# Three heads' gated outputs transposed by 32x32 blocks and a trip through memory, and the first transposes of the probabilities issued before the next scores

## The chip, the cores and the metric

The kernel is one program on one core of a Trainium2 chip. The core has five engines that each run their own list of instructions in order and wait for one another through semaphores: PE (TensorE, matrix products and transposes by a product with the identity, results to PSUM), DVE (VectorE), ACT (ScalarE), POOL (GpSimd) and SP (SyncE, which here only issues DMAs). PEld is the row of the profile that shows the loading of PE's stationary operand; it runs beside PE.

The metric is the device time of one execution in microseconds (us). The kernel before was timed three times: 1155.04, 1155.28 and 1155.72 us, median 1155.28. Its profiled execution took 1155.31 us, of which 1153.3 us lie between the first and the last instruction that the profile shows (the span). All times of rows below are in us from the start of that span, unless marked ns.

## The reference, cut to what matters

Two layers over 512 tokens of width 1024. Layer 1 is retention with four heads, chunked, here computed for all 512 tokens at once; layer 2 is attention with four groups of four heads, each head over all earlier tokens of two branches (selected blocks, which at this length are all of them, and a window of 512), plus a compressed branch.

```python
def retention_layer(h, g_norm, w_in, gn_gain, w_out):
    proj = rmsnorm(h, g_norm) @ w_in
    q, k, v, gate = jnp.split(proj, [...], axis=-1)
    ...
    o = retention_chunkwise(q, k, heads(v, RET_V_DIM))
    o = (o - mu) * lax.rsqrt(var + EPS) * gn_gain
    y = (jax.nn.silu(gate) * o).astype(h.dtype) @ w_out
    return h + y

def nsa_query_block(q, gates, blk, k_cmp, v_cmp, k_sel, v_sel, k_win, v_win):
    ...
    p_s = softmax(where(valid_s, q @ ks * scale, NEG)); o_s = p_s @ vs
    ...
    p_w = softmax(where(valid_w, q @ kw * scale, NEG)); o_w = p_w @ vw
    return gates[..., 0:1] * o_c + gates[..., 1:2] * o_s + gates[..., 2:3] * o_w
```

## The kernel before, in words

**Products.** Every operand of a product is held as a high and a low part in a four-byte format; `mm3` (L349) issues three products per pair (high-high, high-low, low-high). Weights come through one stream of 512 KB pieces: `Stream.load` issues the DMA on SP into one of four raw buffers, POOL multiplies a gain in where the piece needs one (L176, two halves), ACT writes the high part (L190, or L194 by slices with the gain) and DVE the low part (L205, or L209). `W.tick()` does one such step ahead of need; `W.tick(2)` does two.

**Order.** Nothing is scheduled by a tool: the order in which the code is written is the order on each engine. PSUM has eight banks under four tags: "d" two banks, "s" three, "pt" two, "o" one. A bank under a tag is taken in turn, and the product that writes it again waits until DVE or ACT has read what was there.

**Layer 1.** For head h the code computes q and k (`proj_rot`, four calls of 24 products of 128x512, the results read from "d" by `rot_mul` on DVE), then adds the output projection of head h-1 (`out_proj`), then v, the scores, the gate and the output of head h (`retention_out`, whose last instruction, L514 on POOL, leaves y = gate times the normalized output in `gate[:, t]`, 128 tokens by 512). The output projection needs y with its features on the partitions. `retention_yT(t)` does this: four PE transposes of 128x128 into a "pt" bank (L519), then `split_psum` (ACT copies the high part, DVE subtracts the low part) into `yH` and `yL`. For heads 1 to 3 these four calls (for the head before) stand between the calls of `proj_rot`; for the last head they stand after the loop.

**Layer 2.** The loop at L1034 runs over four groups and eight steps u in each; u = 2h + b is head h and branch b. One step holds: `scores(next)` for the following step (products into three "s" banks; DVE adds the mask, L942 and L945, and takes the row maximum, L947; ACT takes the exponential into `P`, L954); up to three fillers from a list (`fill(0)`, `fill(1)`, `fill(2)`: pieces of projections of 12 products each, which go to "d" banks); `scale_probs(next)` (DVE reciprocal, L963, then POOL scales the four parts of `P`, L967); `probs_T(u, 0)` and `probs_T(u, 1)`, the PE transposes of the scaled probabilities of this step (L976: eight into both "pt" banks, then two into one) with their splits (ACT L364, DVE L365) into `tH`, `tL`; `W.tick(2)`; in even steps `cmp_T(h)`, four more transposes into "pt" (L906), read by ACT (L909) and DVE (L910); then `values(u)`, the products of probabilities and values into "o" (L355, in odd steps first one of L984), read in odd steps by DVE and ACT (L993 to L995).

**Fillers.** What the three fillers are depends on the step. A gate or query projection is two fillers that fill one "d" bank, read by ACT and DVE (L752 and L753, L739 and L740) after the second. A piece of the output projection of the group before (`pair_tiles`) is two fillers that each fill two "d" banks, read by DVE (L1015). Seven steps have pieces of an output projection as both of the first two fillers: step 5 of group 0, steps 1 and 5 of groups 1 to 3. Steps with only two fillers have none between `cmp_T` and `values`: steps 0 to 3 and 7 of group 0, step 7 of groups 1 and 2, and steps 2, 4, 6 and 7 of group 3; step 3 of group 3 has one.

Of the kernel before, what the change touches and what calls it, by code (L numbers as in the profile page):

```python
# [11 lines left out]
F32 = mybir.dt.float32  # L12
F32R = mybir.dt.float32r
BF = mybir.dt.bfloat16
AF = mybir.ActivationFunctionType
# [221 lines left out]
def decoder(ctx: ExitStack, tc: tile.TileContext, x, xT, stream, cst, msk, gains, fnorm, out):  # L237
    nc = tc.nc
    pe, act, dve, pool = nc.tensor, nc.scalar, nc.vector, nc.gpsimd
    ctx.enter_context(tc.manual_schedule())  # L240
    sb = ctx.enter_context(tc.tile_pool(name="sb", bufs=1))
    ps = ctx.enter_context(tc.tile_pool(name="ps", bufs=1, space=bass.MemoryType.PSUM))
    nF = 4096 + 1024 * RAWS + 700 + 8192
    nR = 8192 + 2048 * SLOTS + 15104
# [4 lines left out]
    def V(o, n):  # L249
        assert o + n <= nF, (o, n)  # L250
        return arenaF[:, o:o + n]
# [12 lines left out]
    fb = 4096 + 1024 * RAWS  # L264
# [44 lines left out]
    yH = R(rb + 10752, 2048).rearrange("p (c n) -> p c n", c=4)  # L309
    yL = R(rb + 12800, 2048).rearrange("p (c n) -> p c n", c=4)  # L310
# [3 lines left out]
    cs = V(fb + 4096, 1024).rearrange("p (a n) -> p a n", a=2)  # L314
    dec = V(fb + 5120, 1024).rearrange("p (h n) -> p h n", h=2)
    yb = [V(fb + 6144 + 512 * i, 512) for i in range(2)]
    rx = V(fb, 4096).rearrange("p (k t n) -> p k t n", k=NK, t=NT)


# [5 lines left out]
    o = psum("o")  # L325
# [83 lines left out]
    def proj_rot(h, b, c):  # L409
        p = W.get("rin", 0, 1024, b + 256 * h + 128 * c, 128)  # L410
        o = psum("s" if h == 0 and b else "d")
        wst(p, o, 0, 4)
        if h or c == 0:
            W.tick()
        wst(p, o, 4, 8)
        p.done()
        if h == 0:
            return o
        rot_mul(o, c)
# [6 lines left out]
    def rot_split(H, L):  # L426
        pool.tensor_sub(rot[:, 0], rot[:, 0], rot[:, 3])
        pool.tensor_add(rot[:, 1], rot[:, 1], rot[:, 2])
        for i in range(2):
            c = slice(512 * i, 512 * i + 512)  # L430
            act.activation(H[:, c], rot[:, i], AF.Copy)
            dve.tensor_sub(L[:, c], rot[:, i], H[:, c].bitcast(F32))
# [83 lines left out]
    def retention_yT(t, bank="pt"):  # L516
        p = psum(bank)
        for c in range(4):
            pe.transpose(p[:, 128 * c:128 * c + 128], gate[:, t, 128 * c:128 * c + 128], ident)  # L519
        p3 = p.rearrange("p (c n) -> p c n", c=4)  # L520
        c = slice(128 * t, 128 * t + 128)
        split_psum(yH[:, :, c], yL[:, :, c], p3)

    def out_tile(t, c, p, YH, YL):
        o = psum("s" if t % 2 else "d")
        for a in range(2):
            mm3(o, [(YH[:, 2 * a + k, 128 * t:128 * t + 128], YL[:, 2 * a + k, 128 * t:128 * t + 128],
                     p[a].h[:, k], p[a].l[:, k]) for k in range(2)], a == 0, a == 1)
        d = hacc[:, t, 512 * c:512 * c + 512]
        dve.tensor_add(d, d, o)  # L530
# [15 lines left out]
    for h in range(HEADS):  # L546
        if h == 0:
            p = [W.get("rin", 0, 1024, 128 * c, 128) for c in (0, 1)]
            o = [psum("d") for c in (0, 1)]
            for k in range(NK):  # L550
                for c in (0, 1):
                    wst(p[c], o[c], k, k + 1)
                if k % 4 == 3:
                    W.tick()
            for c in (0, 1):
                p[c].done()
            dve.tensor_copy(masks, yb[0][:, :M_END])
            o += [proj_rot(h, 1024, c) for c in (0, 1)]
            rotary_scale()
            for b in range(2):  # L560
                for c in range(2):
                    rot_mul(o[2 * b + c], c)
                rot_split(*((kH, kL) if b else (qH, qL)))
        else:
            proj_rot(h, 0, 0)
            retention_yT(0)
            retention_yT(1)
            proj_rot(h, 0, 1)
            rot_split(qH, qL)
            retention_yT(2)  # L570
            retention_yT(3)
            proj_rot(h, 1024, 0)
            proj_rot(h, 1024, 1)
            rot_split(kH, kL)
            run(out_proj("rout", h - 1, yH, yL))
        tokens("rin", h, 2048, v_evac, ("o", "s", "pt", "pt") if h == 0 else ("d", "d", "s", "s"))
        retention_scores(h)
        if h < 3:
            load_decay(h + 1)
        tokens("rin", h, 4096, g_evac, ("d", "d", "pt", "pt"))  # L580
        for t in range(NT):
            retention_out(t)
# [258 lines left out]
    p = v_pieces(0)  # L841
# [127 lines left out]
    def probs_T(u, part, tag="pt"):  # L969
        Pu = P[u % 2]  # L970
        for j0, bank in (((0, (0,)), (1, (1, 3))), ((2, (2,)),))[part]:
            p = psum(tag)
            f = 0
            for j in bank:
                for i in range(j, NT):
                    pe.transpose(p[:, f:f + 128], Pu[:, PO[i] + 128 * j:PO[i] + 128 * j + 128], ident)  # L976
                    f += 128
            c = slice(TO[j0], TO[j0] + f)
            split_psum(tH[:, c], tL[:, c], p[:, :f])
# [54 lines left out]
    for g in range(GROUPS):  # L1034
        f = fillers(g)
        for u in range(8):
            h = u // 2
            last = (g, u) == (3, 7)
            W.auto = False
            left = 2 * len(between(g, h))  # L1040
            first = 4 if h == 3 else left // 2
            n = PLAN[u] if g == 3 else left - first if u % 2 else first
            steps = [1, 1, 0] if last else PARTS[n]

            def fill(i):
                for _ in range(steps[i]):
                    next(f)

            sums = None
            if u < 7:  # L1050
                nxt = g, u + 1
            elif g < 3:
                k_proj(g + 1, 0)
                k_proj(g + 1, 1)
                nxt = g + 1, 0
            else:
                nxt = None
            if g == u == 0:
                fill(0)
            if nxt:  # L1060
                sums, chain = scores(*nxt)
            if g or u:
                fill(0)
            if sums is not None:
                scale_probs(*nxt, sums)
            probs_T(u, 0)
            next(chain, 0)
            fill(1)
            probs_T(u, 1, "pt" if steps[1] else "d")
            W.tick(0 if last else 2)  # L1070
            next(chain, 0)
            if u % 2 == 0:
                cmp_T(h)
            fill(2)
            if u % 2 == 0:
                o_head = psum("o")
            values(g, u, o_head)
            W.auto = True
        run(f)
        if g < 3:  # L1080
            p = v_pieces(g + 1)
            for t in range(NT):
                v_proj(g + 1, t, p, ("d", "pt")[t % 2], t % 2)
# [101 lines left out]
```

## Time and profile before

| | |
|---|---|
| Median of three runs | 1155.28 us |
| Profiled execution, device time | 1155.31 us |
| Its span | 1153.3 us |
| PE busy | 1132.1 us (98%), 5812 products and transposes |
| DVE busy | 710.4 us (62%) |
| ACT busy | 486.7 us (42%) |
| POOL busy | 317.4 us (28%) |
| Memory traffic | 101.90 MB, mean 88 GB/s |
| PE transposes of L519 (y) | 64, of which 48 before the last head's |
| PE transposes of L976 (probabilities) | 320, in 32 steps |

A matrix product's row starts when it starts and ends when its last result is out, so rows that follow each other overlap; how long PE takes for a piece of work is read here from the start of its row to the start of the next row of PE. In brackets at the end of a row stands how long the engine had been idle before it, and who ended that.

### The profile page before, as it was taken

Reading aid. Unit: us, or ns where it says so; the run is one execution under the profiler, and the core shown is the slowest. Engines: PE = TensorE matmul, PEld = TensorE weight load, DVE = VectorE, ACT = ScalarE, POOL = GpSimd, SP = SyncE. Lnnn points to the kernel's source line nnn. Section 1 sums busy time; section 2 is a strip of 40 time slices with the busy share of each in tenths; the row PEclk is TensorE's granted clock in tenths of the full one; section 3 lists DMA queues with packets and bytes.
Section 4 is the critical chain, followed back from the end, with each engine's and each line's share of the span. In section 5 each row is a group of like instructions: output and inputs, shape, how many; then the busy total and the mean of one; then the engine's idle time right before and its main releaser. Section 6 shows DMA issues by size and latency. Waiting matters only on the chain. (4 is left out here: it accounts for less than half of the span.)

```text
span 1153.3 us, 15259 instructions
## 1 busy us (share of the span) xinstructions
PE 1132.1 (98%) x5812; PEld 964.3 (84%) x5812; DVE 710.4 (62%) x1226; ACT 486.7 (42%) x916; POOL 317.4 (28%) x357
## 2 busy tenths in 40 slices
PE   9999999999999999999899999999999999999997
PEld 7888888888888888988777889888898888988886
DVE  4746435544634665656577865778468774788555
ACT  6433223223323454545455433444345443444653
POOL 0212003002200212346645332354153431421012
PEclk9999999999999999999999999999999999999999
DMA  8422331222232123244531211222031211221211
GB/s 329 149 97 73 110 101 55 92 101 74 86 116 73 55 78 106 73 152 160 163 110 56 74 37 39 78 85 66 27 93 55 74 56 44 85 85 44 74 37 73
DMA packets 29593, 101.90 MB, mean 88 GB/s; under 512 B 3536, under 2 KB 3792, under 8 KB 29520
## 3 DMA queue, kind: packets, MB, share of 16 engines
q1 hardware_dynamic: 29088, 100.15, 26.8%
q8 instruction: 45, 0.74, 0.3%
q10 hardware_dynamic: 432, 0.79, 0.2%
q14 instruction: 28, 0.23, 0.1%
HBM read 98.83 MB, written 2.10 MB: 88 GB/s over the span
## 5 line engine op out<-in xcount | busy, mean ns | idle before, releaser
L355 PE MATMUL d<-arenaR 128*128 128x512 f32 (+2 forms) x2904 | 676.5, 386 | 2.4 <-ACT arenaR L136 1.0
L355 PEld LDWEIGHTS d<-arenaR 128*128 128x128 f32 x2904 | 524.5, 188 | 103.2 <-DVE arenaF L753 1.4
L355 PE MATMUL s<-arenaR 128*128 128x512 f32 (+8 forms) x1182 | 239.8, 354 | 0.7 <-ACT arenaR L364 0.5
L205 DVE TENSOR_TENSOR arenaR<-arenaF,arenaR 128x1024 fp32r<-128x1024 f32 (+1 forms) x142 | 191.7, 1369 | 70.5 <-ACT arenaR L190 70.3
L355 PEld LDWEIGHTS s<-arenaR 128*128 128x128 f32 x1182 | 200.3, 188 | 30.6 <-ACT arenaR L364 0.7
L190 ACT ACTIVATE arenaR<-arenaF 128x1024 fp32r<-128x1024 f32 (+1 forms) x142 | 145.8, 1048 | 105.6 <-PE s L355 68.4
L176 POOL TENSOR_TENSOR arenaF<-arenaF 128x512 f32<-128x512 f32 x108 | 135.3, 1276 | 99.2 <-DMA arenaF<-stream_dram 94.7
L355 PE MATMUL o<-arenaR 128*128 128x512 f32 (+3 forms) x744 | 128.8, 322 | 6.3 <-DVE arenaR L792 4.1
L967 POOL TENSOR_SCALAR arenaF<-arenaF 128x512 f32<-128x512 f32 (+3 forms) x128 | 67.2, 545 | 232.3 <-ACT arenaR L364 118.8
L355 PEld LDWEIGHTS o<-arenaR 128*128 128x128 f32 x744 | 114.3, 189 | 19.6 <-DVE arenaR L792 5.1
L954 ACT ACTIVATE arenaF<-s,arenaF 128x512 f32<-128x512 f32 (+3 forms) x128 | 67.1, 526 | 101.4 <-DVE arenaF L947 90.6
L365 DVE TENSOR_TENSOR arenaR<-pt,arenaR 128x512 fp32r<-128x512 f32 (+1 forms) x141 | 82.9, 618 | 36.9 <-ACT arenaR L364 34.3
L364 ACT ACTIVATE arenaR<-pt 128x512 fp32r<-128x512 f32 (+1 forms) x141 | 70.8, 541 | 73.3 <-PE pt L976 35.2
L371 POOL TENSOR_TENSOR arenaF<-arenaF 128x1 f32<-128x1 f32 (+1 forms) x25 | 14.2, 570 | 295.3 <-DVE arenaF L370 295.3
L355 PE MATMUL pt<-arenaR 128*128 128x512 f32 (+1 forms) x384 | 75.9, 349 | 0.0
L355 PEld LDWEIGHTS pt<-arenaR 128*128 128x128 f32 x384 | 62.7, 188 | 9.4
L209 DVE SCALAR_TENSOR_TENSOR arenaR<-arenaF,arenaR 128x512 fp32r<-128x512 f32 x64 | 45.7, 763 | 35.1 <-PE pt L355 21.4
L194 ACT ACTIVATE arenaR<-arenaF 128x512 fp32r<-128x512 f32 x64 | 43.1, 720 | 46.7 <-issue 22.3
L947 DVE TENSOR_REDUCE arenaF<-s 128x1 f32<-128x512 f32 (+3 forms) x128 | 59.9, 489 | 3.3
L1015 DVE TENSOR_TENSOR arenaF<-arenaF,d 128x512 f32<-128x512 f32 x64 | 42.4, 683 | 8.6 <-PE d L355 7.8
L976 PEld LDWEIGHTS pt<-arenaF 128*128 128x128 f32 x318 | 38.3, 141 | 10.7 <-DVE arenaR L365 3.1
L976 PE MATMUL pt<-arenaF 128*128 128x128 f32 x318 | 45.1, 273 | 1.9 <-DVE arenaR L365 1.9
(126 smaller groups left out, 704.8 us busy)
## 6 DMA issues: line engine op xcount, KB each, us to landing
arenaF<-stream_dram SPq DMA_DIRECT2D x174, 512.0 KB, 3.6
arenaF<-xT_dram SPq DMA_DIRECT2D x8, 256.0 KB, 5.3
arenaF<-x_dram SPq DMA_DIRECT2D x4, 512.0 KB, 8.4
out_dram<-arenaF SPq DMA_DIRECT2D x3, 512.0 KB, 2.6
arenaF<-cst_dram SPq DMA_DIRECT2D x4, 256.0 KB, 3.9
arenaF<-stream_dram ACTq DMA_DIRECT2D x2, 256.0 KB, 4.2
arenaF<-stream_dram SPq DMA_DIRECT2D x2, 256.0 KB, 5.9
arenaF<-cst_dram SPq DMA_DIRECT2D x1, 512.0 KB, 9.5
```

Source lines behind the costliest of these rows:

```text
L176: self.nc.gpsimd.tensor_mul(r3[:, k], r3[:, k], g[:, k, None].to_broadcast([128, m // 2, w]))
L190: self.nc.scalar.activation(hi[:, :m * w], raw, AF.Copy)
L194: self.nc.scalar.activation(hi[:, c], raw[:, c], AF.Copy, scale=g[:, k:k + 1])
L205: self.nc.vector.tensor_sub(lo[:, :m * w], raw, hi[:, :m * w])
L209: self.nc.vector.scalar_tensor_tensor(lo[:, c], raw[:, c], g[:, k:k + 1], hi[:, c], op0=OP.mult, op1=OP.subtract)
L355: pe.matmul(o, a, b, start=start and i == 0, stop=stop and i == n - 1)
L364: act.activation(h, src, AF.Copy)
L365: dve.tensor_sub(l, src, h.bitcast(F32))
L947: dve.reduce_max(mx[:, i:i + 1], o[:, f:f + 128 * i + 128], axis=mybir.AxisListType.X, negate=True)
L954: act.activation(Pu[:, PO[i]:PO[i] + n], o[:, f:f + n], AF.Exp, bias=mx[:, i:i + 1], accum_out=sm_[:, i:i + 1])
L967: pool.tensor_scalar(w, w, sm_[:, i:i + 1], 1.0, op0=OP.mult, op1=OP.mult)
L976: pe.transpose(p[:, f:f + 128], Pu[:, PO[i] + 128 * j:PO[i] + 128 * j + 128], ident)
```

## The change

It has two parts.

**Layer 1, heads 0 to 2** (transposed while heads 1 to 3 start). The 16 PE transposes per head and the reads of their PSUM banks are gone. In their place DVE transposes `gate[:, t]` in blocks of 32x32 into a buffer `yt` (four instructions of 128x512 per head, in two calls of `retention_blocks`), and SP moves the blocks: four DMAs of 128 KB per call write `yt` to memory in an order in which the blocks stand where they belong, and one DMA of 512 KB per call (`retention_back`) reads them back into `gate`. `retention_split` then takes the high part (ACT) and the low part (DVE) from there. The first call for each half stands earlier than the PE transposes' splits did, the splits after `proj_rot(h, 1024, 0)` and `proj_rot(h, 1024, 1)`. Both calls of `retention_blocks` write the same `yt`, so DVE's second pair waits until the first four DMAs have read it.

**Layer 2, all 32 steps.** `probs_T(u, 0)` stands at the head of the step, ahead of `scores(next)` and the first filler. (The first step of all had its first filler ahead of the scores; there too it now follows them.)

```diff
+    yt = V(fb + 7168, 1024)
...
+    def retention_blocks(i):
+        for t in range(2):
+            dve.transpose(view(yt, 128 * t, (32, 4), (256, 4), (1, 32)),
+                          view(gate, 512 * (2 * i + t), (128, 4), (32, 4), (1, 32)))
+        m = moved[i] = dr.tile([128, 1024], F32, name="moved")
+        for a in range(4):
+            nc.sync.dma_start(bass.AP(tensor=m.tensor, offset=m.offset + 256 * a,
+                                      ap=[[1024, 32], [32 * 1024, 4], [1, 256]]),
+                              yt[32 * a:32 * a + 32].rearrange("p (b n) -> p b n", b=4))
+
+    def retention_back(i):
+        nc.sync.dma_start(gate[:, 2 * i:2 * i + 2].rearrange("p t n -> p (t n)"), moved[i])
+
+    def retention_split(t):
+        src = view(gate, 1024 * (t // 2) + 128 * (t % 2), (32, 4), (256, 4), (1, 32))
+        c = slice(128 * t, 128 * t + 128)
+        h, l = (y[:, :, c].rearrange("p c (a n) -> p c a n", a=4) for y in (yH, yL))
+        act.activation(h, src, AF.Copy)
+        dve.tensor_sub(l, src, h.bitcast(F32))
...
             proj_rot(h, 0, 0)
-            retention_yT(0)
-            retention_yT(1)
+            retention_blocks(0)
             proj_rot(h, 0, 1)
+            retention_blocks(1)
+            retention_back(0)
             rot_split(qH, qL)
-            retention_yT(2)
-            retention_yT(3)
+            retention_back(1)
             proj_rot(h, 1024, 0)
+            retention_split(0)
+            retention_split(1)
             proj_rot(h, 1024, 1)
+            retention_split(2)
+            retention_split(3)
             rot_split(kH, kL)
             run(out_proj("rout", h - 1, yH, yL))
...
-            if g == u == 0:
-                fill(0)
+            probs_T(u, 0)
             if nxt:
                 sums, chain = scores(*nxt)
-            if g or u:
-                fill(0)
+            fill(0)
             if sums is not None:
                 scale_probs(*nxt, sums)
-            probs_T(u, 0)
             next(chain, 0)
             fill(1)
```

In the lists below a row is a line, an operation, what it writes and reads (with the number of the buffer, which only tells one from another), a shape and a count. The lines of the changed kernel are two higher in the shared helpers and 34 higher in layer 2 (L365 is L367 there, L945 is L979, L976 is L1010, L1015 is L1049).

PE at the start of head 2 (d: q and k, pt: the transposes of y, s: the first output tile of the other bank). Before:

```order
L355 MATMUL o_1250<-arenaR_64 128x512 x12
L355 MATMUL d_1269<-arenaR_64 128x512 x24
L519 MATMUL pt_1303<-arenaF_63 128x128 x4
L519 MATMUL pt_1310<-arenaF_63 128x128 x4
L355 MATMUL d_1317<-arenaR_64 128x512 x24
L519 MATMUL pt_1355<-arenaF_63 128x128 x4
L519 MATMUL pt_1362<-arenaF_63 128x128 x4
L355 MATMUL d_1369<-arenaR_64 128x512 x24
L355 MATMUL d_1400<-arenaR_64 128x512 x24
L355 MATMUL d_1436<-arenaR_64 128x512 x12
```

Now:

```order
L357 MATMUL o_1248<-arenaR_66 128x512 x12
L357 MATMUL d_1267<-arenaR_66 128x512 x24
L357 MATMUL d_1308<-arenaR_66 128x512 x24
L357 MATMUL d_1355<-arenaR_66 128x512 x24
L357 MATMUL d_1390<-arenaR_66 128x512 x24
L357 MATMUL d_1430<-arenaR_66 128x512 x12
```

The two groups of eight transposes are gone; the four projections and the first output tile (d_1430) follow each other.

PE in group 1, from the end of step 0's values (o) into step 1 (s: the next scores, pt: the first transposes, d: the first two fillers, two banks each). Before:

```order
L355 MATMUL o_5354<-arenaR_64 128x256 x3
L355 MATMUL s_5367<-arenaR_64 128x512 x3
L355 MATMUL s_5374<-arenaR_64 128x416 x3
L355 MATMUL s_5374<-arenaR_64 128x32 x3
L355 MATMUL s_5385<-arenaR_64 128x160 x3
L355 MATMUL s_5385<-arenaR_64 128x288 x3
L355 MATMUL d_5400<-arenaR_64 128x512 x6
L355 MATMUL d_5408<-arenaR_64 128x512 x6
L976 MATMUL pt_5422<-arenaF_63 128x128 x4
L976 MATMUL pt_5429<-arenaF_63 128x128 x4
L355 MATMUL d_5437<-arenaR_64 128x512 x6
L355 MATMUL d_5445<-arenaR_64 128x512 x6
```

Now:

```order
L357 MATMUL o_5344<-arenaR_66 128x256 x3
L1010 MATMUL pt_5357<-arenaF_65 128x128 x4
L1010 MATMUL pt_5364<-arenaF_65 128x128 x4
L357 MATMUL s_5371<-arenaR_66 128x512 x3
L357 MATMUL s_5378<-arenaR_66 128x416 x3
L357 MATMUL s_5378<-arenaR_66 128x32 x3
L357 MATMUL s_5389<-arenaR_66 128x160 x3
L357 MATMUL s_5389<-arenaR_66 128x288 x3
L357 MATMUL d_5404<-arenaR_66 128x512 x6
L357 MATMUL d_5412<-arenaR_66 128x512 x6
L357 MATMUL d_5427<-arenaR_66 128x512 x6
L357 MATMUL d_5435<-arenaR_66 128x512 x6
```

The eight transposes stand ahead of the scores; the two fillers, which use the two "d" banks twice, now follow each other.

DVE in the same step (L945 to L951 read the next scores, L889 and L890 begin the compressed branch, L1015 reads the "d" banks of the first filler). Before:

```order
L945 TENSOR_TENSOR s_5367<-s_5367,masks_65 128x128
L947 TENSOR_REDUCE arenaF_63<-s_5367 128x1
L945 TENSOR_TENSOR s_5374<-s_5374,masks_65 128x128
L947 TENSOR_REDUCE arenaF_63<-s_5374 128x1
L951 TENSOR_TENSOR arenaF_63<-s_5374,masks_65 128x64
L942 TENSOR_TENSOR s_5385<-s_5385,masks_65 128x2x128
L947 TENSOR_REDUCE arenaF_63<-s_5385 128x1 x2
L951 TENSOR_TENSOR arenaF_63<-s_5385,masks_65 128x64
L889 TENSOR_REDUCE arenaF_63<-arenaF_63 128x4
L890 TENSOR_TENSOR arenaF_63<-arenaF_63 128x128
L1015 TENSOR_TENSOR arenaF_63<-arenaF_63,d_5400 128x512
L1015 TENSOR_TENSOR arenaF_63<-arenaF_63,d_5408 128x512
```

Now:

```order
L367 TENSOR_TENSOR arenaR_66<-pt_5364,arenaR_66 128x512
L979 TENSOR_TENSOR s_5371<-s_5371,masks_67 128x128
L981 TENSOR_REDUCE arenaF_65<-s_5371 128x1
L979 TENSOR_TENSOR s_5378<-s_5378,masks_67 128x128
L981 TENSOR_REDUCE arenaF_65<-s_5378 128x1
L985 TENSOR_TENSOR arenaF_65<-s_5378,masks_67 128x64
L976 TENSOR_TENSOR s_5389<-s_5389,masks_67 128x2x128
L981 TENSOR_REDUCE arenaF_65<-s_5389 128x1 x2
L985 TENSOR_TENSOR arenaF_65<-s_5389,masks_67 128x64
L923 TENSOR_REDUCE arenaF_65<-arenaF_65 128x4
L924 TENSOR_TENSOR arenaF_65<-arenaF_65 128x128
L1049 TENSOR_TENSOR arenaF_65<-arenaF_65,d_5404 128x512
```

The first row of the second list is the later of the split's two subtractions. Both stood behind the reads of the first filler and the reciprocal; now they stand ahead of all that DVE does for the next scores, and the reads of "d" come behind that.

## Rows read from the trace of the kernel before

**Rows 1.** Busy time by stretch: stretch, length, PE, PEld, DVE, ACT, POOL.

```profile
600.00:1081.00 481.00, 476.64 (x2658) 413.77 (x2657) 340.62 (x701) 216.53 (x497) 170.39 (x216) 1.00 0.20 63
727.00:992.00 265.00, 264.81 (x1475) 230.72 (x1474) 186.55 (x375) 115.64 (x263) 99.28 (x122) 1.00 0.21 65
```

**Rows 2.** Waits of PE's weight loads, 600 to 1082 us: total, times, longest.

```profile
PEld pt L976 <- DVE arenaR L365: 3.1, 3, 1.5
PEld pt L906 <- POOL arenaF L967: 1.8, 4, 0.5
PEld d L355 <- DVE arenaF L753: 1.4, 1, 1.4
```

**Rows 3.** Instructions in order of time, start of head 2: start, length.

```profile
184.42 5.61 PE L355 MATMUL d<-arenaR 128*128 128x512 f32 x24
...
189.86 1.03 PE L519 MATMUL pt<-arenaF 128*128 128x128 f32 x8
...
190.65 5.72 PE L355 MATMUL d<-arenaR 128*128 128x512 f32 x24
...
205.34 1.22 DVE L205 TENSOR_TENSOR arenaR<-arenaF,arenaR 128x1024 fp32r<-128x1024 f32 x1
```

**Rows 4.** DMA issues: size of one, median us from issue to landing.

```profile
out_dram<-arenaF SPq DMA_DIRECT2D x1, 256.0 KB, 2.3
...
arenaF<-msk_dram SPq DMA_DIRECT2D x1, 128.0 KB, 7.0
```

**Rows 5.** In order of time, group 1, step 1 (736.4 to 745.1 us).

```profile
736.39 2.49 PE L355 MATMUL s<-arenaR 128*128 128x512 f32 x15
737.28 0.30 DVE L945 TENSOR_TENSOR s<-s,masks 128x128 f32<-128x128 f32 x1 [0.51 <-PE s L355]
...
738.72 2.94 PE L355 MATMUL d<-arenaR 128*128 128x512 f32 x12
...
740.93 1.46 DVE L1015 TENSOR_TENSOR arenaF<-arenaF,d 128x512 f32<-128x512 f32 x2
...
741.49 1.03 PE L976 MATMUL pt<-arenaF 128*128 128x128 f32 x8
...
742.28 3.00 PE L355 MATMUL d<-arenaR 128*128 128x512 f32 x12
...
742.82 1.29 DVE L365 TENSOR_TENSOR arenaR<-pt,arenaR 128x512 fp32r<-128x512 f32 x2
```

**Rows 6.** In order of time, ends of steps 0 and 2 of group 0, 2 of group 3.

```profile
609.51 2.49 PE L355 MATMUL s<-arenaR 128*128 128x512 f32 x15
...
609.94 0.69 DVE L910 TENSOR_TENSOR arenaR<-pt,arenaR 32x512 fp32r<-32x512 f32 x1
...
631.50 3.02 POOL L176 TENSOR_TENSOR arenaF<-arenaF 128x512 f32<-128x512 f32 x2
631.52 4.08 DVE L205 TENSOR_TENSOR arenaR<-arenaF,arenaR 128x1024 fp32r<-128x1024 f32 x2
...
633.20 2.50 PE L355 MATMUL s<-arenaR 128*128 128x512 f32 x15
...
635.64 0.69 DVE L910 TENSOR_TENSOR arenaR<-pt,arenaR 32x512 fp32r<-32x512 f32 x1
...
1025.85 2.50 PE L355 MATMUL s<-arenaR 128*128 128x512 f32 x15
...
1027.43 0.69 DVE L910 TENSOR_TENSOR arenaR<-pt,arenaR 32x512 fp32r<-32x512 f32 x1
```

**Rows 7.** In order of time, last value projection before group 1, then the scores.

```profile
722.79 2.10 PE L355 MATMUL s<-arenaR 128*128 128x512 f32 x12
...
723.41 0.42 DVE L365 TENSOR_TENSOR arenaR<-pt,arenaR 128x256 fp32r<-128x256 f32 x1 [1.51 <-ACT arenaR L364]
```

**Rows 8.** In order of time, end of step 3 of group 3.

```profile
1032.87 3.03 POOL L967 TENSOR_SCALAR arenaF<-arenaF 128x512 f32<-128x512 f32 x4 [9.08 <-ACT arenaR L364]
...
1035.32 2.08 PE L355 MATMUL s<-arenaR 128*128 128x512 f32 x12
```

More of the change, by code (lines that the diff above doesn't have):

```diff
@@ L241, in decoder @@
     sb = ctx.enter_context(tc.tile_pool(name="sb", bufs=1))
+    dr = ctx.enter_context(tc.tile_pool(name="dr", bufs=2, space=bass.MemoryType.DRAM))
     ps = ctx.enter_context(tc.tile_pool(name="ps", bufs=1, space=bass.MemoryType.PSUM))
@@ L522, in retention_yT, with view @@
         split_psum(yH[:, :, c], yL[:, :, c], p3)
+    def view(a, o, *ap):
+        return bass.AP(tensor=a.tensor, offset=a.offset + o, ap=[list(a.ap[0])] + [list(d) for d in ap])
+    moved = [None, None]
+    def retention_blocks(i):
[15 more added lines that the diff above has]
+        dve.tensor_sub(l, src, h.bitcast(F32))
     def out_tile(t, c, p, YH, YL):
```

## The prediction

> **What bounds the kernel now.** I read the stages first. In layer 2's loop PE is idle for 4.4 of 481 us, and in groups 1 and 2 for 0.2 of 265 us, while DVE is busy for 71% of the loop [rows 1]. So the time there is what PE issues: work that leaves another engine gains nothing, and a new wait of PE costs its full length. Second come PE's waits in that loop; three kinds make 6.3 us [rows 2]. Third, the order of time around each place that the change touches, to see how much cover is left. The chain of waits says only that PE is the chain. What the reader should see: the first part takes work from PE, the second leaves PE's work as it is and can only take or add waits.
>
> **Layer 1.** PE spends 0.79 us on eight transposes (189.86 to 190.65) [rows 3]. Six such groups go: -4.7 us.
>
> What replaces them must arrive before PE wants y. One of DVE's block transposes is not in the trace; the nearest rows bound it by 0.65 us (half of the pair of 1.29 us for 128x512) [rows 5] and 1.22 us (128x1024) [rows 3]. I take 0.65, as the size is that one's. A transfer of the trip is bounded by 2.3 and 7.0 us [rows 4]; I take 2.3, since the 7.0 stands alone in the crowded start. The chain, with 5.44 us for a projection of 24 products (184.42 to 189.86) [rows 3]: the first q is complete at 189.86, and two reads of it, two low parts and the first pair of block transposes take six times 0.65, to 193.8. Their writes land at 196.1. The second pair waits for them (one `yt`) and for the second q (195.3, read until 196.6), and ends at 197.9. Only then does SP, in order, issue the second writes and the first read, which lands at 200.2; the second read lands at 202.5, and SP's next weights wait behind it until its issue at 200.2. ACT and DVE need about 1.4 us for a split. PE wants the first of y after four projections, at 206.2, so some 4 us are left, and for its third quarter at about 211. Cost nothing. Behind DVE's wait for `yt` stand the split of q and the next read of "d", both wanted only later than the waits that I price. At 4.9 us a transfer the cover is gone; at 7.0 the first of y is 4 us late in each of three heads.
>
> The Trainium skill (DMA: Bandwidth & Descriptors, section Anatomy of one DMA) gives a DMA a fixed part of about 2 us, most of it the receipt from the memory that is written. The row of 2.3 us agrees; with an estimate of some 3 us for four times 128 KB by that page the trip still ends in time, and the sum stays.
>
> **Layer 2: waits that go.** The second transposes and `cmp_T` wait for a "pt" bank whose reader stands behind the next scores on DVE; one filler waits for a late read of "d". With the first transposes early all of it can go: -6.3 us [rows 2], and at least nothing.
>
> **Layer 2: a new wait for "d".** In group 1, step 1 PE now does eight transposes (0.79), the scores (736.39 to 738.72, 2.33), the first filler (to 741.49, 2.77), and reaches the second filler where it did, at 742.3 [rows 5]. DVE's subtractions end 2.62 us after the transposes start (741.49 to 742.82 + 1.29), so at 739.0. Only then can L945 begin, which began at 737.28: 1.73 us later. All behind it on DVE follows, so the first read of a "d" bank moves from 740.93 to 742.66, and ends 0.7 us later, at 743.4. The second filler needs that bank: PE waits 1.05 us. Seven steps have this pair of fillers: +7.4 us, with bounds of 0.8 and 1.2 each.
>
> **Layer 2: a new wait for "pt".** After an even step the later four of the eight transposes need the bank of `cmp_T`. L910 frees it, and stands behind `W.tick(2)` on DVE. Where no filler lies between `cmp_T` and the values, PE is there first: at the end of the values (where the scores start now) plus 0.4 us for the first four. L910 ends at 610.63, 636.33 and 1028.12, PE comes at 609.91, 633.60 and 1026.25 [rows 6]: 0.7, 2.7 and 1.9 us. Until now the scores covered this. Two more such places, at the start of steps 5 and 7 of group 3, I take at the least of the three. Sum +6.7 us, bounds 5 and 9.
>
> The long one comes from two low parts that took 4.08 us with POOL's gains beside them [rows 6], where one alone takes 1.22 [rows 3]. The Trainium skill (SBUF — State Buffer, section SBUF: two separate sides) says that DVE with two inputs from SBUF and POOL hold a shared port in turn and lock each other out. The trace agrees in direction. By that rule layer 1's new subtractions, which now read SBUF twice, can each be held up by a POOL instruction too; that does not change the sum, as they have the cover named above.
>
> **Layer 2: behind the value projections.** At the start of groups 1 to 3 the later four transposes need the "pt" bank of the last value projection. It is read until 723.83, and PE would come at 723.19 (722.79 + 0.4) [rows 7]: 0.64 us three times, +1.9 us; bounds 0 and 2.5.
>
> **Layer 2: what follows.** One wait of each of the first two kinds of rows 2 falls in step 0 of group 0; with them gone PE is about 0.8 us earlier, but L910 is not, so step 1 gives it back: +0.8. In step 2 DVE's work for the scores is later by two subtractions (1.29) [rows 5], and L910 with it: +1.3. Step 4 of group 3 now begins with transposes, which need POOL's scaling. That ended at 1035.90, with PE at 1035.32, so 0.6 us late already [rows 8]; the scores ahead of it are later on DVE by up to 2 us, and I take +1.5. In the same step the wait for L753 (1.4) [rows 2], counted as gone, comes back, as the exponentials ahead of it on ACT are later: +1.4. Sum +5.0, bounds 2 and 8.
>
> **Sum.** -4.7 - 6.3 + 7.4 + 6.7 + 1.9 + 5.0 = +10.0 us on the profiled execution's 1155.31 us (its span of 1153.3 and 2.0 around it; the median of the runs is within 0.03): 1165.3 us. All bounds on one side would give 1157 or 1178.
>
> **The rivals.**
>
> *DVE makes up the lateness.* DVE has 29% idle time [rows 1]. If its subtractions end about 1 us earlier than worked out, the seven waits for "d" vanish and most of what follows with them; the waits for "pt" stay: -4.7 - 6.3 + 6.7 + 1.9 = -2.4, so 1152.9 us, faster. Against it: DVE stood idle for 0.51 us ahead of L945 [rows 5], so the 2.62 us are latency and not a queue that could shrink. It holds if PE waits under 0.3 us ahead of the second filler in group 1, step 1.
>
> *It nets out.* If the two low parts take 1.22 us each, because POOL's work falls elsewhere, the long wait shrinks by 1.6; with the low bounds of the "d" waits (5.6), of the value projections (0) and of what follows (2) the sum is -4.7 - 6.3 + 5.6 + 5.1 + 2 = +1.7: 1157.0 us, not to be told from no change. For it: an engine that waits less elsewhere; against it: four terms must be low at once.
>
> *The trip is late.* At 7.0 us a transfer PE waits 4 us or more in three heads, on top of the forecast: 1178 us or more. Against it: three transfers in a row at the bound.
>
> *The change doesn't do what it says.* The order has the transposes ahead; but where PE waits there for POOL's scaling they come no earlier. That is so in group 3, step 4, and in the sum.
>
> **How the numbers follow.** Forecast 0.70, made up 0.15, nets out 0.10, late trip 0.05. The forecast's own range is 1158 to 1172. The made-up case reaches down to 1147, the late trip past 1178; a range of 1153 to 1173 leaves out about half of the first and all of the last, and the forecast's tails, some 17 in 100. A difference under 0.2% (2.3 us) is not to be told from none. Faster by more than that: nearly all of the made-up case, 0.14. Slower by more: the forecast, the late trip and a little of the netting, 0.77. The same: 0.09.
>
> **What would show it.** Right: at the start of heads 1 to 3 PE's products follow each other without transposes or a gap; in step 1 of groups 1 to 3 PE waits about 1 us ahead of the second filler for the read of "d"; in group 0, step 3 it waits 2 to 4 us between the first and the later four transposes, for the last subtraction of `cmp_T`. Wrong: PE's idle time in the loop stays under 5 us (then DVE was quick enough), or PE waits ahead of the first output tile of heads 1 to 3 (then the trip is the bound), or `cmp_T`'s subtraction ends ahead of the values in steps with two fillers.

## The result, and the profile after

The changed kernel took 1170.26 us (median of four runs, 1169.70 to 1172.27) against 1155.16 us for the kernel before (four runs): ratio 1.0133, 95% interval 1.0115 to 1.0151, so 13.3 to 17.4 us slower. The profiled execution, at 1172.27 us, is the longest of the four. The forecast had the sign, and with 1165.3 us two thirds of the size; its range of 1153 to 1173 holds the time.

PE issues 48 transposes less (5764 products and transposes for 5812) and its row of the page reads 97% (98% before). The page's first two lines, then the loop of layer 2 and groups 1 and 2 by stretch, to be held against [rows 1] (stretch, length, PE, PEld, DVE, ACT, POOL):

```profile
span 1170.5 us, 15222 instructions
## 1 busy us (share of the span) xinstructions
PE 1133.6 (97%) x5764; PEld 962.2 (82%) x5764; DVE 719.8 (61%) x1238; ACT 487.5 (42%) x916; POOL 326.5 (28%) x357
```

```profile
598.30:1098.10 499.80, 483.43 (x2668) 419.01 (x2668) 341.43 (x705) 217.58 (x499) 177.07 (x216) 0.99 0.19 61
727.70:997.40 269.70, 265.53 (x1474) 230.87 (x1473) 185.60 (x372) 115.16 (x260) 109.17 (x124) 1.00 0.20 63
```

Groups 1 and 2 took 265 us with 0.2 us of idle time before; they now take 269.7 with 4.2 idle, for the same work. The waits of PE's weight loads in the loop, which answer to [rows 2] (total, times, longest):

```profile
PEld d L357 <- DVE arenaF L1049: 8.3, 7, 1.2
PEld pt L1010 <- DVE arenaR L944: 5.7, 4, 1.9
PEld pt L1010 <- POOL arenaF L1001: 4.4, 4, 2.4
PEld pt L1010 <- DVE arenaR L367: 2.2, 3, 0.7
PEld d L357 <- DVE arenaF L787: 1.1, 1, 1.1
```

Of the old kinds only the last is left (L787 is L753 before). The fourth row has the name of the first of [rows 2], but its three waits stand at the starts of groups 1 to 3. The first, second and fourth are the three new kinds of the forecast, in their order; the third, POOL's scaling, had a small place in it.

Where the time went can be read step by step. I took the start of PE's first row after the values of each step in both traces; the difference of the lengths is what a step costs. Steps that are not named changed by less than 0.15 us.

| Steps (group, step) | Longer by, us |
|---|---|
| 0,5; 1,1; 1,5; 2,1; 2,5; 3,1 | 0.99 to 1.03 each |
| 3,5 | 1.79 |
| step 0 of groups 1, 2, 3 | 0.69 each |
| 0,1 and 0,2 and 0,3 | 1.18, 1.69, 2.61 |
| 0,4 and 1,2 | -1.27, -0.38 |
| 3,3 and 3,7 | 2.16, 1.51 |

From the end of step 0 of group 0 to the last values the loop is 17.5 us longer (488.9 for 471.4). Step 3 of group 0 holds almost no wait of PE: its 2.61 us are transposes and products at the lower level of the granted clock (last section). Ahead of the loop the profiled execution stood 0.3 us earlier than before. Layer 1 ended only 1.4 us earlier (541.56 for 542.95, the same product), for 4.7 forecast, and 1.1 us of that were lost again on the way to the loop (last section).

**Layer 1.** In order of time at the start of head 2 (SPq is the issue of DMAs on SP), to be held against [rows 3]:

```profile
192.16 1.46 DVE L536 STREAM_TRANSPOSE arenaF<-arenaF 128x512 f32<-128x512 f32 x2
...
193.65 2.29 SPq L540 DMA_DIRECT2D moved<-arenaF  x4
...
198.63 1.53 DVE L536 STREAM_TRANSPOSE arenaF<-arenaF 128x512 f32<-128x512 f32 x2 [2.27 <-DMA moved<-arenaF]
...
200.19 1.75 SPq L540 DMA_DIRECT2D moved<-arenaF  x4
...
202.11 2.44 SPq L545 DMA_DIRECT2D arenaF<-moved  x2
...
205.78 1.15 ACT L551 ACTIVATE arenaR<-arenaF 128x512 fp32r<-128x512 f32 x2 [4.43 <-DMA arenaF<-moved]
...
206.46 3.29 PE L357 MATMUL d<-arenaR 128*128 128x512 f32 x12 [0.55 <-ACT arenaR L551]
```

DVE was on time with the first pair (192.16 to 193.62; 193.8 forecast), and a block transpose cost 0.71 us (0.65 taken). The four writes of a call, which SP issues one after another, needed 4.98 us from their first issue to DVE's release (193.65 to 198.63). SP then issued the second four (1.75 us) ahead of the first read, which took 3.7 us (202.11 to 205.78). So PE came to the output tile before y did.

**Group 1, step 1**, the place of [rows 5]:

```profile
741.99 1.04 PE L1010 MATMUL pt<-arenaF 128*128 128x128 f32 x8
742.78 2.58 PE L357 MATMUL s<-arenaR 128*128 128x512 f32 x15
745.20 2.91 PE L357 MATMUL d<-arenaR 128*128 128x512 f32 x12
748.89 3.02 PE L357 MATMUL d<-arenaR 128*128 128x512 f32 x12 [0.79 <-DVE arenaF L1049]
```

```profile
743.32 1.29 DVE L367 TENSOR_TENSOR arenaR<-pt,arenaR 128x512 fp32r<-128x512 f32 x2 [1.12 <-ACT arenaR L366]
744.52 0.29 DVE L979 TENSOR_TENSOR s<-s,masks 128x128 f32<-128x128 f32 x1
...
748.15 1.28 DVE L1049 TENSOR_TENSOR arenaF<-arenaF,d 128x512 f32<-128x512 f32 x2
```

L979 starts 1.74 us after the scores do, for 0.89 us before (737.28 - 736.39); the first read of "d" comes 5.37 us after the scores' start, for 4.54. The second filler starts 3.69 us after the first; without a wait it is 2.77.

### The profile page after: what moved, and what is told of

It reads as the page before. It is cut to its first block, busy times and chain, and to the rows that moved or that the text cites. A ratio compares the mean times of both kernels' runs of the same rounds, so it can differ in the third digit from the quotient of the medians.

```text
span 1170.5 us, 15222 instructions
## 1 busy us (share of the span) xinstructions
PE 1133.6 (97%) x5764; PEld 962.2 (82%) x5764; DVE 719.8 (61%) x1238; ACT 487.5 (42%) x916; POOL 326.5 (28%) x357
## 5 line engine op out<-in xcount | busy, mean ns | idle before, releaser
L357 PE MATMUL s<-arenaR 128*128 128x512 f32 (+8 forms) x1182 | 243.9, 357 | 0.7 <-ACT arenaR L366 0.5
L176 POOL TENSOR_TENSOR arenaF<-arenaF 128x512 f32<-128x512 f32 x108 | 141.8, 1333 | 88.7 <-DMA arenaF<-stream_dram 84.3
L1001 POOL TENSOR_SCALAR arenaF<-arenaF 128x512 f32<-128x512 f32 (+3 forms) x128 | 71.8, 580 | 257.1 <-DVE arenaF L998 223.7
L366 ACT ACTIVATE arenaR<-pt 128x512 fp32r<-128x512 f32 (+1 forms) x129 | 65.0, 533 | 108.7 <-PE pt L1010 70.2
L367 DVE TENSOR_TENSOR arenaR<-pt,arenaR 128x512 fp32r<-128x512 f32 (+1 forms) x129 | 75.5, 611 | 46.2 <-ACT arenaR L366 45.5
L1010 PE MATMUL pt<-arenaF 128*128 128x128 f32 x318 | 48.0, 278 | 9.7 <-DVE arenaR L944 4.7
L1010 PEld LDWEIGHTS pt<-arenaF 128*128 128x128 f32 x318 | 38.0, 142 | 16.7 <-DVE arenaR L944 5.7
L1049 DVE TENSOR_TENSOR arenaF<-arenaF,d 128x512 f32<-128x512 f32 x64 | 42.0, 684 | 15.4 <-PE d L357 15.1
```

The source lines that it names most:

```text
L176: self.nc.gpsimd.tensor_mul(r3[:, k], r3[:, k], g[:, k, None].to_broadcast([128, m // 2, w]))
L357: pe.matmul(o, a, b, start=start and i == 0, stop=stop and i == n - 1)
L366: act.activation(h, src, AF.Copy)
L367: dve.tensor_sub(l, src, h.bitcast(F32))
L1001: pool.tensor_scalar(w, w, sm_[:, i:i + 1], 1.0, op0=OP.mult, op1=OP.mult)
```

## The experiments

Each was timed over five rounds against the kernel before on the same chip (medians there 1155.01, 1154.44 and 1154.93 us in three sets). A step's length is taken as above.

**1. Layer 1's part alone.** The loop of layer 2 is that of before.

> Layer 1's part of the change alone; layer 2 is in the order of the kernel before. In the changed kernel's trace PE waits 3.3 us in total, three times, at the first output tile of heads 1 to 3 for the high part of y that came back from memory. If that is the trip's price: 4.7 us of transposes less 3.3 us of waits, 1.4 us faster than before, 1153.8 us, and the three waits stand in the profile at about 1.1 us each. Rival (the waits came from the other part of the change or from that one execution): no waits there, 4.7 us faster, 1150.5 us.

**2. Two buffers for the blocks.**

```diff
-    yt = V(fb + 7168, 1024)
+    yt2 = [V(fb + 7168, 1024), V(fb + 6144, 1024)]
...
     def retention_blocks(i):
+        yt = yt2[i]
```

> As the one before, but the two calls of the block transposes write two different buffers (the second one is yb, which is free by then), so DVE's second pair no longer waits 2.27 us for the first four writes to memory. If that wait is what makes the trip late, the second pair, its writes and both reads come some 2 us earlier, the waits of 1.1 us at heads 1 to 3 vanish, and the time is 4.7 us under before: 1150.5 us. Rival (the transfers themselves, or SP's order, are what is late): the waits stay above 0.5 us each, 1152.5 us or more.

Measured: 1153.60 us for the first (0.9986, 0.9974 to 0.9997), 1149.04 us for the second (0.9950, 0.9938 to 0.9963). PE's waits for y in heads 1 to 3, first run and then second:

```profile
PEld d L357 <- ACT arenaR L551: 4.5, 3, 1.7
PEld d L357 <- DVE arenaR L552: 1.3, 3, 0.4
```

```profile
PEld d L357 <- DVE arenaR L553: 0.6, 2, 0.4
```

And the trip of the second, in order of time at the same head:

```profile
190.21 1.45 DVE L537 STREAM_TRANSPOSE arenaF<-arenaF 128x512 f32<-128x512 f32 x2
...
191.69 1.75 SPq L541 DMA_DIRECT2D moved<-arenaF  x4
...
194.33 1.45 DVE L537 STREAM_TRANSPOSE arenaF<-arenaF 128x512 f32<-128x512 f32 x2
...
195.81 1.82 SPq L541 DMA_DIRECT2D moved<-arenaF  x4
197.80 3.09 SPq L546 DMA_DIRECT2D arenaF<-moved  x2
...
202.81 1.16 ACT L552 ACTIVATE arenaR<-arenaF 128x512 fp32r<-128x512 f32 x2 [3.41 <-DMA arenaF<-moved]
```

DVE's second pair starts 4.1 us after the first, not 6.5, and ACT gets y before PE wants it. The one buffer was what made the trip late; the transfers themselves were not too slow for the cover. With the trip in time the part gains some 5.0 us: the product at 542.95 before starts at 541.79 to 543.26 in the six traces whose layer 1 is that of before (mean 542.52), and at 537.22 to 537.64 in the three with two buffers (this one and those of experiment 8; mean 537.48). That is 0.84 us for each group of eight transposes, near the 0.79 that I had read from start to start.

**3. Layer 2's part alone.** Layer 1 is that of before.

> Layer 2's part alone; layer 1 is that of the kernel before. The steps of layer 2's loop are together 17.5 us longer in the changed kernel's trace. If nothing of that comes from layer 1: about 16.5 us slower than before, 1171.7 us, with seven waits of about 1.0 us ahead of the second filler for the read of d. Rival (part of it follows from layer 1, for instance from the clock or the weights' stream): under 1168 us.

Measured: 1170.91 us (1.0142, 1.0128 to 1.0156), with the loop's waits within 0.2 us of those of the changed kernel. So the two parts add: 15.9 us slower and 1.4 faster make 14.5, for 15.1 of both.

**4. Early transposes, late splits.** With `later`, `probs_T` only notes its splits, and they are done behind the reciprocal.

```diff
+            later = []
-            probs_T(u, 0)
+            probs_T(u, 0, later=later)
...
             if sums is not None:
                 scale_probs(*nxt, sums)
+            for a in later:
+                split_psum(*a)
```

> As the one before, PE's first transposes are early, but ACT's and DVE's split of them stands where it stood before the change (behind the next scores, the first filler's reads and the reciprocal). If the seven waits for d come from DVE's subtractions standing ahead of its work for the scores, they vanish (-7.1 us); the waits for pt behind cmp_T and behind the value projections stay (0.7, 2.7 and 1.9 us, the starts of steps 5 and 7 of group 3, three times 0.7), and some of the old waits for pt come back (0 to 3 us): 1162 to 1166 us. Rival (two fillers that follow each other on PE wait for d whatever DVE's order): the seven waits stay, 1170 us or more.

Measured: 1168.30 us (1.0123, 1.0107 to 1.0139), above the range that I had given. The five largest kinds of its waits in the loop:

```profile
PEld pt L976 <- DVE arenaR L910: 9.0, 5, 2.8
PEld d L355 <- DVE arenaF L1018: 3.3, 7, 0.5
PEld pt L976 <- DVE arenaR L365: 2.2, 3, 0.7
PEld pt L976 <- issue: 2.0, 3, 1.6
PEld pt L906 <- POOL arenaF L967: 1.9, 6, 0.4
```

Six of the seven steps fell from about 1.02 to between 0.24 and 0.28 us longer than before, and the seventh, which also holds a wait for "pt", by 0.63: three quarters of what they lost is due to where the split stands (ACT's copies moved with DVE's subtractions), since PE's order is the same in both. The rival is out for that part; 0.25 us a step stay, and this run doesn't say what for. But all waits for "pt" banks together grew from 12.2 to 17.3 us. Those for the subtraction of `cmp_T` went from 5.6 to 9.0, of which 2.8 in step 3 of group 0 take the place of a wait for POOL there in experiment 3; old kinds came back besides. What was saved at the "d" banks was given back at the "pt" banks, which I had expected only as old waits of 0 to 3 us. Step 3 of group 0 is 4.2 us longer than before; some 1.5 of that are the lower clock (0.50 for 3.4 us from 636.2).

**5. `cmp_T` ahead of the weights.**

```diff
-            W.tick(0 if last else 2)
             next(chain, 0)
             if u % 2 == 0:
                 cmp_T(h)
+            W.tick(0 if last else 2)
```

> Layer 2's part alone, as the run with 1170.9 us, but the compressed branch's last step and cmp_T with its reads stand ahead of W.tick(2), so the subtraction that frees cmp_T's pt bank no longer queues behind two low parts on DVE. If that queue is the price, the waits for it go (1.2, 0.3, 1.9, 0.8 and 1.5 us at the starts of steps 1 and 3 of group 0 and 3, 5 and 7 of group 3): 5.7 us less, 1165.2 us; the 2.3 us at step 3 of group 0, which the profile puts down to POOL's scaling, stay. Rival (cmp_T now makes PE wait for POOL's product instead, or POOL's scaling takes the place of each wait): 1168 us or more.

Measured: 1167.54 us (1.0108, 1.0092 to 1.0124), between the two. The two largest kinds of its waits in the loop, and group 0, step 2 of it; then that step in the changed kernel:

```profile
PEld d L355 <- DVE arenaF L1015: 8.6, 7, 1.2
PEld pt L976 <- POOL arenaF L967: 3.0, 4, 1.4
```

```profile
632.22 2.06 POOL L967 TENSOR_SCALAR arenaF<-arenaF 128x512 f32<-128x512 f32 x4 [3.58 <-ACT arenaR L739]
...
633.18 0.69 DVE L910 TENSOR_TENSOR arenaR<-pt,arenaR 32x512 fp32r<-32x512 f32 x1
633.90 3.42 DVE L205 TENSOR_TENSOR arenaR<-arenaF,arenaR 128x1024 fp32r<-128x1024 f32 x2
```

```profile
632.11 4.07 POOL L1001 TENSOR_SCALAR arenaF<-arenaF 128x512 f32<-128x512 f32 x4 [2.79 <-ACT arenaR L773]
...
632.96 2.60 DVE L205 TENSOR_TENSOR arenaR<-arenaF,arenaR 128x1024 fp32r<-128x1024 f32 x2
...
635.60 0.69 DVE L944 TENSOR_TENSOR arenaR<-pt,arenaR 32x512 fp32r<-32x512 f32 x1
635.77 0.18 PEld L1010 LDWEIGHTS pt<-arenaF 128*128 128x128 f32 x1 [2.38 <-POOL arenaF L1001]
635.78 2.21 PE L1010 MATMUL pt<-arenaF 128*128 128x128 f32 x8 [2.18 <-POOL arenaF L1001]
```

The waits for `cmp_T`'s subtraction are gone from the list, and the steps behind them are shorter by 1.23 (0,1), 1.65 (3,3), 0.79 (3,5) and 1.51 us (3,7). The wait for POOL at step 3 of group 0 shrank from 2.65 to 0.7 us, against what I expected: POOL's four scalings take 4.07 us beside DVE's low parts and 2.06 us without them, so the order on DVE had set POOL's time as well. What is missing to 1165.2 is mostly step 4 of group 3, 2.0 us longer than in experiment 3, and a wait of 0.9 us for a weight's low part ahead of group 2. At step 4 the transposes come to POOL's scaling earlier and wait 2.3 us for it instead of 1.7 (the rival, at one place); behind that the clock falls to 0.50 for 3.4 us, and the scores take 3.0 us for 2.0.

**6. The value projection in "d".**

```diff
-                v_proj(g + 1, t, p, ("d", "pt")[t % 2], t % 2)
+                v_proj(g + 1, t, p, ("pt", "d")[t % 2], t % 2)
```

> Layer 2's part alone, as the run with 1170.9 us, but the last value projection ahead of groups 1 to 3 is written to a d bank, so both pt banks are free sooner. If the three waits of 0.66 us at the start of these groups come from that bank, they vanish: 1168.9 us. Rival (the transposes there wait for something else, such as the scaled probabilities): 1170.9 us, the waits stay.

Measured: 1169.56 us (1.0124, 1.0110 to 1.0138). By medians against experiment 3 that is inside the spread; by the steps it is plain: the three steps are 0.71 us shorter each, and the wait for a "pt" bank released by the split's subtraction (2.2 us, three times, as in the changed kernel) is no longer among the loop's waits. One new wait of 0.9 us at the start of step 3 of group 2 took a part of it back. Step 3 of group 0, up to whose end the code is that of experiment 3, is 1.0 us shorter than in experiment 3: the clock is at 0.50 there for 3.4 us and not for 6.8.

**7. All three mended** (the edits of 4, 5 and 6 together).

> Layer 2's part with early transposes on PE in all steps, and all three prices taken away: the splits in their old place, cmp_T ahead of W.tick(2), and the last value projection of a group in a d bank instead of a pt bank. From 1168.3 us with late splits alone: 9.0 us of waits for the subtraction of cmp_T and 2.0 us behind the value projections go, 0.3 us of waits for d in a dozen steps stay: 1157 to 1160 us. If instead the early transposes cost something that none of the three names, 1164 us or more.

Measured: 1159.44 us (1.0043, 1.0027 to 1.0059), 5.0 us slower than before in its set, where the part without them is 15.9 slower. In its profiled execution the loop is 5.9 us longer than before: seven times 0.24 to 0.29 us (waits for "d"), 2.3 us in step 2 of group 0 and 0.9 ahead of group 2 (again a weight's low part) are the largest pieces. In step 2 PE waits for a "pt" bank that the late split frees, for 1.06 us before, and the clock is at 0.50 for 3.4 us from there:

```profile
632.80 0.66 PE L976 MATMUL pt<-arenaF 128*128 128x128 f32 x2 [2.25 <-DVE arenaR L365]
```

So even then the early order gains nothing over the old one.

**8. Only where it gains.** The blocks with two buffers; early transposes in even steps only, without the first of groups 1 to 3 (first run), then in steps 0, 2 and 4 of group 0 alone (second run).

```diff
+            early = u % 2 == 0 and (g == 0 or u > 0)    # second run: g == 0 and u in (0, 2, 4)
+            if early:
+                probs_T(u, 0)
...
-            probs_T(u, 0)
+            if not early:
+                probs_T(u, 0)
```

> The blocks with two buffers, and in layer 2 the first transposes early only in the even steps (without the first step of groups 1 to 3); the odd steps are in the order of the kernel before. By the step times of the whole change, the waits for d and those for pt behind cmp_T lie all in odd steps, and the even steps only gain: step 0 of group 0 0.8 us, step 2 0.6, step 4 1.3, step 2 of group 1 0.4. So about 3 us under the run with two buffers alone (1149.0): 1146.0 us. Rival (the later subtractions of an even step are paid in the odd step behind it, by the same lateness on DVE or by POOL's scaling): 1149 us or more.

> The blocks with two buffers, and the first transposes early only in steps 0, 2 and 4 of group 0. In the run with all even steps, step 2 gained 1.2 us and step 4 0.7 us, and step 4 of group 3 lost 1.2 us (a query's bank is read 2.0 us late); the other even steps changed by 0.02 us or less. Without the loss: 1.2 us under that run's 1147.9 us, 1146.7 us, faster than before by about 8 us. Rival (the gain of steps 2 and 4 is given back later in the group, or is within the spread of the stage before the loop): 1147.9 us or more.

Measured: 1147.86 us (0.9941, 0.9926 to 0.9957) and 1146.59 us (0.9921, 0.9908 to 0.9935). Against the run with two buffers alone, steps 2 and 4 of group 0 are 1.21 and 0.71 us shorter in the first (1.21 and 0.80 in the second), and the odd steps behind them are not longer: there the next transposes still stand behind the scores. All other even steps are within 0.02 us, but for step 4 of group 3, which is 1.20 us longer in the first run and unchanged in the second. There a gate's bank is read later (L788 is L753 of the kernel before; the expectation calls it a query's), and 0.6 us go to POOL's scaling. The wait for that read in the loop, in the first run and then in the second:

```profile
PEld d L357 <- DVE arenaF L788: 2.7, 2, 2.0
```

```profile
PEld d L357 <- DVE arenaF L788: 1.9, 2, 1.4
```

The last version is 0.8% faster than the kernel before and 2% faster than the change; the intervals of the two versions overlap, so that the second is the better one rests on the steps.

## Why the prediction was right, and where it was short

**Layer 1, forecast -4.7, found -1.4.** Removed work was sized nearly right (5.0). The step that failed is the price of a transfer, "I take 2.3, since the 7.0 stands alone in the crowded start", and with it "Their writes land at 196.1". One transfer of 128 KB took 2.9 us (median, 2.0 to 3.6), but what counts is a call: four writes in a row and 4.98 us until the buffer was free. The first read landed 5.6 us later than forecast: 2.3 come from the first writes, 2.0 from SP, which issues the second four ahead of the read (the sum had that at nothing), and 1.4 from the read. For the read the page before has a nearer row than those that I took, the weights' pieces:

```profile
arenaF<-stream_dram SPq DMA_DIRECT2D x174, 512.0 KB, 3.6
```

My own point, 4.9 us a transfer for the end of the cover, was met by the writes; I had given the late trip a chance of 0.05. The section of the Trainium skill that the prediction names there (DMA: Bandwidth & Descriptors, Anatomy of one DMA) is on DMAs that POOL issues. Here SP issues them, and the estimate of some 3 us for four is short of the 4.98 measured. The late trip's mechanism was thus real, at 1.1 us a head (1.5 in experiment 1) and not 4, and a sign that I had named for being wrong is there: PE waits ahead of the first output tile of heads 1 to 3. Experiment 2 shows that its lever was the second pair's wait for `yt`.

**Old waits, forecast -6.3.** They went, but for L753's, which came back at 1.1 of 1.4 us, as worked out.

**New wait for "d", +7.4; found 7.1.** Seven steps, 1.05 forecast and 0.99 to 1.03 found where the step holds no other wait. Experiment 4 shows that the split ahead of L945 makes three quarters of it. "DVE makes up the lateness" is out: DVE's idle share of the loop rose from 29 to 32%, and it stood idle for 1.12 us ahead of the subtractions, for latency and not for a queue.

**New wait for "pt", +6.7; found 8.0.** The places were right, but at the largest the cause was another. PE stood 1.2 us at step 1 of group 0 (0.7 forecast), 1.9 at step 3 of group 3 (1.9), 0.8 and 1.5 at its steps 5 and 7 (0.7 each). At step 3 of group 0 it stood 2.3 us ahead of the first transpose and 0.3 ahead of the second, both for POOL's scaling, where I had 2.7 for the subtraction alone. That subtraction ended at 636.29 (635.60 + 0.69), ahead of the fifth transpose, so the wait between the first and the later four, named as a sign of being right, did not come. There the rival's sentence "where PE waits there for POOL's scaling they come no earlier" held at one place more than I had named. It fits what the Trainium skill (SBUF — State Buffer, section SBUF: two separate sides) states, that DVE with two inputs from SBUF and POOL lock each other out; experiment 5 agrees in direction, with 4.07 and 2.06 us for the same four scalings. I had used it for DVE's time and not for POOL's.

**Behind the value projections, +1.9; found 2.0.** Experiment 6 shows the bank.

**What follows, +5.0; found about 3.6 in waits over 0.3 us:** 1.05 in step 2 of group 0, 1.7 at the start of step 4 of group 3, and L753's.

**The clock, which the sum does not name; found some 2.5.** The granted clock falls in step 3 of group 0, behind PE's waits there, and the step's transposes and scores take that much longer (last section). What is then left of the loop's 17.5 us, about 0.6, is not assigned.

So the forecast's mechanism decided. The profiled execution lies 7 us above the forecast (the median 5): 3.3 are the trip, 1.1 the stretch between layer 1 and the loop, and 2.8 the loop, most of it the clock. That the loop's other terms come out so near is in part luck, since "pt" was 1.3 low and what follows 1.4 high. "It nets out" fails with the terms that it needed low.

## What to carry to other kernels

Moving PE work ahead moves its readers too: on an engine that runs in order, each read of a bank goes ahead of all that stood there, and the price is paid at the banks which that work frees (and here, with 2.5 us, by the clock behind the waits). Ask for each early product which bank it writes, who reads that bank last now, and what stands ahead of this reader; where another wait does not hide behind work that was ahead of it (here the even steps of group 0), the early order is worth having, and elsewhere not. A trip through memory is priced by the call, all its DMAs in a row and the buffer held until the last, and a second buffer can take the wait out of it (here 4.6 us by the medians, 1149.04 for 1153.60).

## What the runs showed of the hardware that I had not expected

POOL's scaling doubled beside DVE's low parts (4.07 against 2.06 us), as told above.

SP's issue of the four writes of a call took 1.7 to 2.3 us; the last of four starts 1.3 to 1.4 us after the first.

Ahead of layer 2's loop the granted clock is at its lower level (0.50, 1.2 GHz) for some 3.5 us, after PE has stood idle several times. In the kernel before that fell into 573 to 576 us, with a wait of PE for DVE behind it; in the profiled execution of the change it fell later, into products that nothing waits behind. In experiment 6 it does not fall there at all, in experiment 7 twice. First before, then after (PE's busy time and count, then PEld, DVE, ACT, POOL, the granted clock):

```profile
573.00:576.00 3.00, 3.00 (x8) 2.32 (x8) 0.34 (x1) 1.50 (x3) 3.00 (x3) 0.50 0.44 152
```

```profile
573.00:576.00 3.00, 1.92 (x10) 1.44 (x8) 0.80 (x1) 2.42 (x3) 2.66 (x4) 1.00 0.52 175
580.00:583.00 3.00, 3.00 (x8) 2.32 (x7) 3.00 (x4) 2.43 (x3) 2.80 (x2) 0.50 0.56 173
```

Before, PE then waited 1.61 us for DVE's L792; after, 3.21 us for the same line at full clock, and paid 1.6 us for the products at the lower clock besides. With 0.5 us lost earlier and 0.9 gained behind it, up to the end of step 0 of group 0, that makes the 1.1 us lost ahead of the loop. The two runs of experiment 8 (on two chips) differ by 2.9 us at the end of step 0 of group 0, and by less than 0.1 at the end of layer 1, with the same instructions up to there; so this stage alone makes 2 to 3 us between executions, more than several of the effects here, and only the lengths of steps tell those apart.

In the loop the clock falls too, in the six versions with early transposes in all steps and in none of the other five: each time in step 2 or 3 of group 0, for 3.4 or 6.8 us, behind waits of PE of 1.4 to 2.8 us together (in experiment 5 again in step 4 of group 3). In the changed kernel (first the stretch, then PE from the end of the eight transposes' wait, whose row stands in experiment 5):

```profile
634.30:641.10 6.80, 5.32 (x20) 4.71 (x20) 4.54 (x8) 1.93 (x4) 3.88 (x4) 0.50 0.47 154
```

```profile
637.63 4.18 PE L357 MATMUL s<-arenaR 128*128 128x512 f32 x15
641.65 5.63 PE L357 MATMUL d<-arenaR 128*128 128x512 f32 x24
```

The scores take 4.02 us from start to start, for 2.33 before (633.20 to 635.53), and the transposes 1.85 (635.78 to 637.63) for 0.79, of which 0.3 are the wait for POOL: some 2.5 us lost to the clock. The time of an execution goes with its mean granted clock: the five of experiment 4 took 1166.82 us at 0.997, 1167.11 at 0.996, 1168.30 and 1169.99 at 0.995, and 1171.43 at 0.993.
